# Seven block products in more row pairs of the down and output products, four banks for the first projections, and the key transposes moved in one decoder layer

## The chip, the core and the metric

The kernel runs on one core of a Trainium2 chip. The metric is device time in microseconds (us), the median of several runs. The engines are named by their functions: TensorE (PE, with PEld for its weight loads), VectorE (DVE), ScalarE (ACT), GpSimd (POOL) and SyncE (SP), which issues most DMA transfers.

## What is computed

The reference is one decoder layer over 256 rows of 2048 numbers, in float32:

```python
h = x
h = h + 0.5 * swiglu(rms_norm(h, ffn1_norm), ffn1_w_gate, ffn1_w_up, ffn1_w_down)
p = rms_norm(h, mix_norm) @ w_in
y_rwkv = rwkv7_time_mix(p[..., :RWKV_IN], ...)     # 16 heads of 64
y_lru  = rglru_mix(p[..., RWKV_IN:], ...)          # gated recurrence, then its own rms_norm
h = h + concatenate([y_rwkv, y_lru]) @ w_out
h = h + 0.5 * swiglu(rms_norm(h, ffn2_norm), ffn2_w_gate, ffn2_w_up, ffn2_w_down)
return rms_norm(h, final_norm)
```

The hidden width of the two feed-forward parts is 5632, so a down product sums over 44 row tiles of 128, and the output product over 16.

## The kernel before

**Products.** Every large product is made of three TensorE products, because each float32 operand is held as a high part (a cast) and a low part (the rest): high by high, high by low, low by high (`three`, L146). A weight tile is loaded by SP into `wst`, ScalarE casts it to `whi` (L96 or L115), and VectorE takes the difference into `wlo` (L97 or L116). Three buffers exist of each (`wpool`), and the loading and splitting of weights has a high priority (offset 4000) in the order that a planner makes of the program.

**Pairs.** `rows_times_pairs` (L153) takes two row tiles of weights, 1024 columns wide, at a time. A pair is a two by two by two block product: two row tiles by two halves of the tokens by two halves of 512 columns. A plan string says how each pair is done. In a plain pair (`n`) eight block products are made, 24 matmuls, into four banks `own`. In a pair of kind `S` seven are made, 21 matmuls, from sums of blocks: VectorE makes the sums of weight blocks (L136 to L138), and seven blocks instead of four are split into high and low parts; sums of the activation blocks come from `block_sums` (L297). Four of the seven products go to four more banks, `aux`, which add up over all S pairs and are added in once at the end (`shared_h`, L334).

**Order of stages.** `ffn` runs the gate and the up product in chunks of 1024 columns, both with three S pairs of eight, then the down product in pieces. In the first feed-forward part there are two pieces of 1024 columns with four S pairs of 22 each. In the second there is one such piece and then two pieces of 512 columns without S pairs (`rows_times`, L180). The transposes of the last chunk's hidden values (`hidden_T`, L274, L280) come after the third pair of the first down piece, and they make the activation sums of the last four pairs there.

**Mixing.** `mix_layer` runs eleven projections of `w_in` (`project`, L610; 256-column matmuls at L199 to L201), which take turns on banks 0 to 2, and between them the recurrence work in an order written out by hand (`order`). `keys_T` (L783, transposes at L792) is the last call of step `r`. The rows that come out are split into the tiles `xahi` and `xalo` (`split_rows`, L1022, L1023): row tiles 0 to 3 and 4 to 7 are the recurrence heads, row tiles 8 to 15 the gated part, which is first scaled by its norm (`lru_norm`, L1017 to L1019; L1087). The same tiles hold the projections' input until the last projection has read them.

**Output product.** `mix_out` (L1091) has two halves of 1024 columns, all sixteen row tiles in order, with `rows_times` on banks 0 to 3 and 4 to 7. After each half the result is added to `h` (L1102), transposed (L229) and split for the second feed-forward part (L237, L238).

**End.** The last piece is added to `h` (L428), its squares are summed (L247), it is multiplied by the final gain (L1238), scaled (L1253, L1256) and written out.

Of the kernel before, what the change touches and what calls it, by code (L numbers as in the profile page):

```python
# [15 lines left out]
ALU = mybir.AluOpType  # L16
# [20 lines left out]
class Core:  # L37
# [115 lines left out]
    def rows_times_pairs(self, mat, c0, plan, ids, own, aux, xhi, xlo, sums, hooks):  # L153
# [3 lines left out]
        for at, (kind, p, w) in enumerate(self.pairs(mat, c0, plan, ids)):  # L157
            first, last = at == 0, at == len(plan) - 1
            if kind == "n":
                for kk in range(2):  # L160
                    for t in range(2):
                        x = [v[:, 2 * p + kk, t * P : (t + 1) * P] for v in (xhi, xlo)]
                        for n in range(2):
                            self.three(own[2 * t + n], x, w[kk][n], first and kk == 0, last and kk == 1)
# [12 lines left out]
            for hook in hooks.get(at, ()):  # L177
                hook()
# [63 lines left out]

    def sumsq(self, c0, w, acc, pool):
# [16 lines left out]
def ffn(core, xhi, xlo, rstd, wg, wu, wd, after_first, after_down, fpool, down, rest, back, spare, head=None):  # L260
# [13 lines left out]
    def hidden_T(c0, w, hid, sums=None):  # L274

        for j in range(0, w // P, 2):
# [14 lines left out]
            if sums:  # L291
                if j == 0:
                    raw = fpool.tile([P, 4, 2, S], F32, name=core.name("hsum"), tag="sg")
                nc.scalar.copy(raw[:, j // 2].rearrange("p k s -> p (k s)"), bk)
                block_sums(raw[:, j // 2], *sums(k // 2))

    def block_sums(r, hi, lo):  # L297

        blk = lambda k, t: r[:, k, t * P : (t + 1) * P]
        nc.vector.tensor_tensor(blk(1, 1), blk(0, 1), blk(1, 1), ALU.add)  # L300
        nc.vector.tensor_tensor(blk(0, 1), blk(0, 0), blk(0, 1), ALU.subtract)
        nc.vector.tensor_tensor(blk(0, 0), blk(1, 1), blk(0, 0), ALU.subtract)
        nc.vector.tensor_tensor(blk(1, 0), blk(1, 0), blk(0, 0), ALU.subtract)
        flat = r.rearrange("p k s -> p (k s)")
        nc.scalar.copy(hi, flat)
        nc.vector.tensor_tensor(lo, flat, hi.bitcast(F32), ALU.subtract)
# [26 lines left out]

    def shared_h(aux, tmp, c0):  # L334

        t1, t2, t3, _ = blocks_of(tmp)
        nc.scalar.copy(t1, aux[0])
        nc.vector.tensor_tensor(t2, aux[2], t1, ALU.add)
        nc.vector.tensor_tensor(t3, aux[3], t2, ALU.add)
        for (t, n), parts in (((0, 1), (aux[1], t2)), ((1, 0), (t3,)), ((1, 1), (aux[1], t3)), ((0, 0), (t1,))):  # L340
            hs = core.h[:, t, c0 + n * 512 : c0 + (n + 1) * 512]
            for part in parts:
                nc.vector.scalar_tensor_tensor(hs, part, 0.5, hs, ALU.mult, ALU.add)
# [5 lines left out]
    for c0, w in chunks:  # L349
# [42 lines left out]
        for i, (k, hi, lo) in enumerate(core.weights([(wu, c0, w)], ks)):  # L392
            core.rows_times(ub, xhi, xlo, k, hi, lo, w, i == 0, i == NK - 1)
            if i % 2 and i // 2 in place:
                block_sums(room(i // 2), *sums(place[i // 2]))
# [5 lines left out]
    hsums = spare()  # L401
    first_s = NF // 2 - 4
    bank0 = 0
    for piece, (c0, w) in enumerate(down):
        nb = w // 512
        if w == 1024:
            own, aux = ([core.bank((bank0 + i) % 8) for i in b] for b in (range(4), range(4, 8)))
            bank0 += 4
            plan = DOWN_PLAN[piece]
            number = {"n": iter(range(first_s)), "S": iter(range(first_s, NF // 2))}  # L410
            ids = [next(number[kind]) for kind in plan]
            hooks = {}
            if pending:
                hooks[DOWN_HIDDEN_AT] = [partial(f, sums=hsums) for f in pending]
            pending = []
            tmp = lambda: fpool.tile([P, NT, 1024], F32, name=core.name("dsh"), tag="hid")
            hooks[plan.rindex("S")] = [lambda: shared_h(aux, tmp(), c0)]
            core.rows_times_pairs(wd, c0, plan, ids, own, aux, hT_hi, hT_lo, hsums, hooks)
            db = [own[0:2], own[2:4]]
        else:  # L420
            db = [[core.bank((bank0 + t * nb + n) % 8) for n in range(nb)] for t in range(NT)]
            bank0 += NT * nb
            for i, (k, hi, lo) in enumerate(core.weights([(wd, c0, w)], list(range(NF)))):
                core.rows_times(db, hT_hi, hT_lo, k, hi, lo, w, i == 0, i == NF - 1)
        for t in range(NT):
            for n in range(nb):
                hs = core.h[:, t, c0 + n * 512 : c0 + (n + 1) * 512]
                nc.vector.scalar_tensor_tensor(hs, db[t][n], 0.5, hs, ALU.mult, ALU.add)  # L428
        after_down(piece)
# [8 lines left out]
class Mix:  # L438
# [171 lines left out]
    def project(self, pieces, ntile, xhi, xlo):  # L610
# [3 lines left out]
        for _ in range((ntile + 1) // 2):  # L614
            bks.append(core.bank(self.nproj % 3))
# [410 lines left out]
def mix_layer(core, dram, xhi, xlo, scratch, nslot):  # L1026
    nc = core.nc
    w_in = dram["w_in"][0]
    with ExitStack() as ctx:
# [20 lines left out]
        def receptance(hf):  # L1050
# [40 lines left out]
def mix_out(core, w_out, yhi, ylo, after_half):  # L1091
    nc = core.nc
    half = core.D // 2
    nb = half // 512
    for hf in range(2):
        db = [[core.bank(4 * hf + t * nb + n) for n in range(nb)] for t in range(core.NT)]
        for i, (k, hi, lo) in enumerate(core.weights([(w_out, hf * half, half)], list(range(core.NK)))):
            core.rows_times(db, yhi, ylo, k, hi, lo, half, i == 0, i == core.NK - 1)
        for t in range(core.NT):
            for n in range(nb):  # L1100
                hs_ = core.h[:, t, hf * half + n * 512 : hf * half + (n + 1) * 512]
                nc.vector.tensor_tensor(hs_, hs_, db[t][n], ALU.add)  # L1102
# [10 lines left out]
def kernel(ctx: ExitStack, tc: tile.TileContext, dram: dict, out: bass.AP):  # L1113
# [32 lines left out]
    def xt_pool(stack, name, **kw):  # L1146
# [10 lines left out]
        return [Halves(half(n, 0), half(n, 1)) for n in ("hi", "lo")], half, sums  # L1157

    with ExitStack() as front:
        xa, xa_half, xa_sums = xt_pool(front, "xa")  # L1160
        with ExitStack() as st:
# [32 lines left out]
            def park(hf):  # L1194
# [8 lines left out]
                first_norm, park, fpool, [(0, HD), (HD, HD)], rest, back, xa_sums, head={q: partial(norm_quarter, q + 1) for q in range(3)})  # L1203
# [11 lines left out]
        xb, _, xb_sums = xt_pool(ctx, "xb", **right)  # L1215
# [5 lines left out]
        mix_out(core, dram["w_out"][0], *xa, half_done)  # L1221
    with ExitStack() as st:
        fpool = st.enter_context(tc.tile_pool(name="ffn2", bufs=1, reuse_waits="tile"))
        down = [(0, HD), (HD, HD // 2), (HD + HD // 2, HD // 2)]
        fb = None

        def closing(piece):
            nonlocal fb
            if piece == 0:
# [4 lines left out]
            c0, w = down[piece]  # L1234
            core.sumsq(c0, w, ssq[3][piece], fpool)
# [4 lines left out]
        def rest2():  # L1240
# [6 lines left out]
            lambda: norm_rows(2, 7, fpool), closing, fpool, down, rest2, back2, xb_sums)  # L1247
# [37 lines left out]
```

## Time and profile before

| | |
|---|---|
| median of 3 runs | 1918.13 us (1918.0 to 1919.51) |
| profiled execution | 1919.43 us, span 1917.7 us |
| TensorE | 10197 matmuls, 1885.3 us busy |
| VectorE | 1513.9 us busy |
| ScalarE | 1012.8 us busy |
| granted TensorE clock | 0.994 of full |
| HBM | 351.25 MB read, 187 GB/s |

The profile is of one execution. The span runs from the first to the last instruction. Busy time of TensorE counts overlapping matmuls from the start of each to its modelled end. Lines such as L97 are lines of the kernel before.

### The profile page before, as it was taken

To read this page: it belongs to the slowest core of one execution; us is meant where nothing else is said; L and a number is where in the kernel's file an instruction comes from. 1 tells how busy PE (TensorE), PEld (TensorE's weight loads), DVE (VectorE), ACT (ScalarE), POOL (GpSimd) and SP (SyncE) were. 2 spreads that over 40 slices of the span, in tenths; PEclk is the share of its full clock that TensorE was granted. 3 is DMA by queue.
4 is the path that set the end of the run, shared out by engine and by line. 5 is a ranking of instruction groups with operands and counts; after the bars stand their busy time and mean duration, and the time that the engine had idled before them with its cause. 6 is when DMAs were issued, how large, how long until landed. Compare 5 with 4: busy or idle time off the path is not lost.

```text
span 1917.7 us, 25761 instructions
## 1 busy us (share of the span) xinstructions
PE 1885.3 (98%) x10197; PEld 1591.7 (83%) x10197; DVE 1513.9 (79%) x1952; ACT 1012.8 (53%) x1232; POOL 9.9 (1%) x53
## 2 busy tenths in 40 slices
PE   7999999999999999999999999999999999999997
PEld 6888888888888889898899978888888888888886
DVE  6889999898867567976595775989898989876653
ACT  6555555555544445544454554655556555554443
POOL 0000000000000001000000000000000000000000
PEclk9999999999999999999999999999999999999999
DMA  6565555555655656645243456555655655756653
GB/s 224 180 206 181 197 198 186 208 186 210 240 200 197 220 192 216 179 122 160 82 154 97 132 197 208 189 198 189 206 193 206 216 176 197 262 199 202 208 189 126
DMA packets 130034, 360.79 MB, mean 188 GB/s; under 512 B 20879, under 2 KB 23128, under 8 KB 129784
## 3 DMA queue, kind: packets, MB, share of 16 engines
q1 hardware_dynamic: 129592, 358.08, 55.6%
q8 instruction: 80, 1.31, 0.3%
q10 hardware_dynamic: 320, 1.06, 0.1%
q14 instruction: 42, 0.34, 0.1%
HBM read 351.25 MB, written 7.86 MB: 187 GB/s over the span
## 4 chain that ended last, share of the span: by engine, by line
PE 83%; DVE 10%; DMA 4%; ACT 1%; issue 1%; SPq 0%; DVEq 0%; ACTq 0%
PE bank L149 17%; PE bank L151 17%; PE bank L150 17%; PE bank L190 5%; PE bank L188 5%; PE bank L187 4%; PE bank L200 4%; PE bank L199 4%; PE bank L201 4%; DVE wlo L116 3%; DMA wst<-in_ffn_w_gate_dram 3%; DVE wlo L97 1%; PE bank L280 1%; PE bank L771 1%; PE bank L699 1%
## 5 line engine op out<-in xcount | busy, mean ns | idle before, releaser
L115 ACT CAST whi<-wst 128x1024 fp32r<-128x1024 f32 (+1 forms) x596 | 589.0, 1001 | 542.7 <-PE bank L151 484.8
L116 DVE TENSOR_TENSOR wlo<-wst,whi 128x1024 fp32r<-128x1024 f32 (+1 forms) x596 | 682.6, 1156 | 146.0 <-ACT whi L115 136.9
L97 DVE TENSOR_TENSOR wlo<-wst,whi 128x1024 fp32r<-128x1024 f32 (+2 forms) x197 | 236.7, 1203 | 150.6 <-ACT whi L96 149.5
L96 ACT CAST whi<-wst 128x1024 fp32r<-128x1024 f32 (+2 forms) x197 | 204.1, 1037 | 258.0 <-PE bank L190 115.7
L199 PE MATMUL bank<-xahi,whi 128*128 128x256 f32 x688 | 198.3, 288 | 2.6 <-DVE raw L629 2.6
L201 PE MATMUL bank<-xahi,wlo 128*128 128x256 f32 x688 | 198.8, 289 | 0.2 <-DVE wlo L97 0.2
L200 PE MATMUL bank<-xalo,whi 128*128 128x256 f32 x688 | 198.7, 289 | 0.0
L149 PE MATMUL bank<-whi,xahi 128*128 128x512 f32 x490 | 191.4, 391 | 0.4 <-DVE hTlo L288 0.4
L149 PE MATMUL bank<-whi,xbhi 128*128 128x512 f32 x490 | 191.2, 390 | 0.4 <-DVE hTlo L288 0.4
L150 PE MATMUL bank<-wlo,xahi 128*128 128x512 f32 x490 | 190.8, 389 | 0.0
L150 PE MATMUL bank<-wlo,xbhi 128*128 128x512 f32 x490 | 190.8, 389 | 0.0
L151 PE MATMUL bank<-whi,xalo 128*128 128x512 f32 x490 | 190.6, 389 | 0.0
L151 PE MATMUL bank<-whi,xblo 128*128 128x512 f32 x490 | 190.6, 389 | 0.0
L149 PE MATMUL bank<-whi,hThi 128*128 128x512 f32 x468 | 182.5, 390 | 0.0
L151 PE MATMUL bank<-whi,hTlo 128*128 128x512 f32 x468 | 182.2, 389 | 0.0
L150 PE MATMUL bank<-wlo,hThi 128*128 128x512 f32 x468 | 182.1, 389 | 0.0
L199 PEld LDWEIGHTS bank<-xahi,whi 128*128 128x128 f32 x688 | 133.4, 194 | 5.7 <-DVE raw L629 2.8
L201 PEld LDWEIGHTS bank<-xahi,wlo 128*128 128x128 f32 x688 | 133.4, 194 | 2.4 <-issue 1.2
L200 PEld LDWEIGHTS bank<-xalo,whi 128*128 128x128 f32 x688 | 133.2, 194 | 2.3 <-issue 1.1
L136 DVE TENSOR_TENSOR wst<-wst 128x1024 f32<-128x1024 f32 x72 | 88.1, 1223 | 28.8 <-DMA wst<-in_ffn_w_up_dram 10.5
L149 PEld LDWEIGHTS bank<-whi,xahi 128*128 128x128 f32 x490 | 92.0, 188 | 20.3 <-PE bank L151 0.8
L149 PEld LDWEIGHTS bank<-whi,xbhi 128*128 128x128 f32 x490 | 92.0, 188 | 19.8 <-PE bank L151 0.8
(345 smaller groups left out, 3011.4 us busy)
## 6 DMA issues: line engine op xcount, KB each, us to landing
wst<-in_ffn_w_up_dram SPq DMA_DIRECT2D x88, 1024.0 KB
wst<-in_ffn_w_down_dram SPq DMA_DIRECT2D x88, 1024.0 KB
wst<-in_ffn_w_gate_dram SPq DMA_DIRECT2D x87, 1024.0 KB
wst<-in_w_in_dram SPq DMA_DIRECT2D x40, 1024.0 KB
wst<-in_w_out_dram SPq DMA_DIRECT2D x16, 1024.0 KB
h<-parked SPq DMA_DIRECT2D x4, 1024.0 KB
wst<-in_w_in_dram SPq DMA_DIRECT2D x4, 640.0 KB
h<-in_x_dram SPq DMA_DIRECT2D x4, 512.0 KB
```

Source lines behind the costliest of these rows:

```text
L96: self.last_split = nc.scalar.copy(hi[:, : m * width], src)
L97: nc.vector.tensor_tensor(lo[:, : m * width], src, hi[:, : m * width].bitcast(F32), ALU.subtract)
L115: self.nc.scalar.copy(hv, src)
L116: self.nc.vector.tensor_tensor(lv, src, hv.bitcast(F32), ALU.subtract)
L149: nc.tensor.matmul(out, a[0], b[0], start=first, stop=False)
L150: nc.tensor.matmul(out, a[0], b[1], start=False, stop=False)
L151: self.last_mm = nc.tensor.matmul(out, a[1], b[0], start=False, stop=last)
L188: nc.tensor.matmul(banks[t][n][:, :w], a, wlo[:, c : c + w], start=False, stop=False)
L190: self.last_mm = nc.tensor.matmul(banks[t][n][:, :w], b, whi[:, c : c + w], start=False, stop=last)
L199: nc.tensor.matmul(out, a, xhi[:, k, :], start=first, stop=False, skip_group_check=True)
L200: nc.tensor.matmul(out, a, xlo[:, k, :], start=False, stop=False, skip_group_check=True)
L201: nc.tensor.matmul(out, b, xhi[:, k, :], start=False, stop=last, skip_group_check=True)
```

## The change

- In both down products, all pieces are now 1024 columns wide and have six S pairs of 22. The activation sums of two more pairs are made by `earlier_sums`, at the start of the first piece, from tiles that are already split. The second feed-forward part has two pieces instead of three.
- The output product uses `rows_times_pairs` with three S pairs of eight in each half. Its activation sums are made from the split rows after all of them, in a new pool. Banks 0 to 3 and 4 to 7 serve as `own` and `aux`, exchanged in the second half.
- In the last pair of every such product the matmuls are sorted so that the first 512 columns are finished before the others, and the closing work of the second feed-forward part is split accordingly.
- The first eight bank allocations of the projections go round four banks instead of three.
- `keys_T` is called at the end of step `v` instead of step `r`.

`block_sums` and `shared_h` become methods of `Core`, unchanged but for a scale. The core of the diff (the pools for the new sums are left out):

```diff
             if kind == "n":
-                for kk in range(2):
-                    for t in range(2):
...
+                turns = itertools.product(range(2), range(2), range(2))
+                for kk, t, n in (sorted(turns, key=lambda v: v[2]) if last else turns):
+                    x = [v[:, 2 * p + kk, t * P : (t + 1) * P] for v in (xhi, xlo)]
+                    self.three(own[2 * t + n], x, w[kk][n], first and kk == 0, last and kk == 1)
...
+    def shared_h(self, aux, tmp, c0, scale):
+        nc = self.nc
+        t1, t2, t3 = (tmp[:, i * 512 : i * 512 + 512] for i in range(3))
+        nc.scalar.copy(t1, aux[0])
+        nc.vector.tensor_tensor(t2, aux[2], t1, ALU.add)
+        nc.vector.tensor_tensor(t3, aux[3], t2, ALU.add)
+        for (t, n), parts in (((0, 1), (aux[1], t2)), ((1, 0), (t3,)), ((1, 1), (aux[1], t3)), ((0, 0), (t1,))):
+            hs = self.h[:, t, c0 + n * 512 : c0 + (n + 1) * 512]
+            for part in parts:
+                nc.vector.scalar_tensor_tensor(hs, part, scale, hs, ALU.mult, ALU.add)
...
-    first_s = NF // 2 - 4
+    first_s = NF // 2 - 6
+    def earlier_sums():
+        for n, p in enumerate(range(first_s, first_s + 2)):
+            pair = slice(2 * p, 2 * p + 2)
+            nc.vector.tensor_tensor(hraw[:, n], hT_hi[:, pair, :].bitcast(F32), hT_lo[:, pair, :].bitcast(F32), ALU.add)
+            core.block_sums(hraw[:, n], *hsums(p))
...
+        if piece == 0:
+            hooks[0] = [earlier_sums]
+            hooks[DOWN_HIDDEN_AT] = [partial(f, sums=hsums) for f in pending]
...
-            bks.append(core.bank(self.nproj % 3))
+            bks.append(core.bank(self.nproj % 4 if self.nproj < 8 else (self.nproj - 8) % 3))
...
             TW[hf] = m.invert_blocks(GR[hf], scratch[hf])
-            BKT[hf] = m.keys_T(BK[hf])
 
         def values(hf):
             V[hf] = shifted(2112 + 512 * hf, 16 + 4 * hf, "v")
+            BKT[hf] = m.keys_T(BK[hf])
...
-def mix_out(core, w_out, yhi, ylo, after_half):
+def mix_out(core, w_out, yhi, ylo, after_half, pool):
...
+    for n, p in enumerate(spairs):
+        raw = pool.tile([P, 2, core.S], F32, name=core.name("ysum"), tag="ysum", bufs=2)
+        pair = slice(2 * p, 2 * p + 2)
+        nc.vector.tensor_tensor(raw, yhi[:, pair, :].bitcast(F32), ylo[:, pair, :].bitcast(F32), ALU.add)
+        core.block_sums(raw, sums[:, n, 0, :], sums[:, n, 1, :])
...
+        own, aux = ([core.bank((4 * hf + i) % 8) for i in b] for b in (range(4), range(4, 8)))
+        core.rows_times_pairs(w_out, hf * half, OUT_PLAN, range(core.NK // 2), own, aux, yhi, ylo, of,
+                              {OUT_PLAN.rindex("S"): [lambda: core.shared_h(aux, tmp(), hf * half, 1.0)]})
...
+OUT_PLAN = "nSnSnSnn"
-DOWN_PLAN, DOWN_HIDDEN_AT = ("nnnnnnSnnnSnnnSnnnSnnn", "nnnSnnnnSnnnnSnnnnSnnn"), 2
+DOWN_PLAN, DOWN_HIDDEN_AT = ("nnnnSnnSnnSnnSnnSnnSnn", "nnSnnSnnSnnSnnSnnSnnnn"), 2
```

## Rows read from the trace of the kernel before

**Rows 1.** The page, part 1: engine, busy us, share of the span, instructions.
```profile
PE 1885.3 (98%) x10197; PEld 1591.7 (83%) x10197; DVE 1513.9 (79%) x1952; ACT 1012.8 (53%) x1232; POOL 9.9 (1%) x53
```
**Rows 2.** Matmuls by start, us long: tiles 0, 8 of half 0; half 1; next stage.
```profile
1098.25 0.40 PE L187 MATMUL bank<-whi,xahi 128*128 128x512 f32 x1
...
1128.51 0.39 PE L187 MATMUL bank<-whi,xahi 128*128 128x512 f32 x1
...
1150.27 0.39 PE L187 MATMUL bank<-whi,xahi 128*128 128x512 f32 x1
...
1195.69 0.39 PE L187 MATMUL bank<-whi,xbhi 128*128 128x512 f32 x1
```
**Rows 3.** Busy time by stretch: a down piece, then around the output product.
```profile
core 0: us, PE busy (x) PEld busy (x) DVE busy (x) ACT busy (x) POOL busy (x), PEclk, DMA share, GB/s
615.00:731.00 116.00, 116.00 (x521) 96.26 (x520) 77.63 (x81) 56.72 (x62) 1.36 (x13) 1.00 0.57 193
1080.00:1094.00 14.00, 14.00 (x112) 13.36 (x110) 14.00 (x12) 7.49 (x9) 0.00 (x0) 1.00 0.28 86
1094.00:1136.00 42.00, 40.94 (x195) 33.05 (x195) 38.39 (x61) 24.02 (x34) 0.11 (x1) 1.00 0.48 156
...
1151.00:1195.00 44.00, 44.00 (x203) 36.42 (x202) 23.72 (x27) 19.39 (x24) 0.00 (x0) 1.00 0.66 216
```
**Rows 4.** VectorE by group, 1094 to 1136 us: x, busy us, mean ns, idle before.
```profile
L97 DVE TENSOR_TENSOR wlo<-wst,whi 128x1024 fp32r<-128x1024 f32 x13 | 15.7, 1208 | 1.8 <-ACT whi L96 1.7
L1087 DVE SCALAR_TENSOR_TENSOR xc<-xc,pc,lss 128x256 f32<-128x256 f32 x8 | 3.4, 475 | 0.0
```
**Rows 5.** VectorE on row tiles 7, 8 to 10 and 12 to 15 of the output product.
```profile
1119.21 0.43 DVE L1023 TENSOR_TENSOR xalo<-y,xahi 128x256 fp32r<-128x256 f32 x1 [0.47 <-ACT xahi L1022]
...
1128.45 1.09 DVE L1023 TENSOR_TENSOR xalo<-xc,xahi 128x256 fp32r<-128x256 f32 x3
...
1134.05 1.42 DVE L1023 TENSOR_TENSOR xalo<-xc,xahi 128x256 fp32r<-128x256 f32 x4
```
**Rows 6.** VectorE around one S pair of a down piece, in order of time.
```profile
536.77 1.23 DVE L136 TENSOR_TENSOR wst<-wst 128x1024 f32<-128x1024 f32 x1 [0.99 <-DMA wst<-in_ffn_w_down_dram]
537.91 1.22 DVE L116 TENSOR_TENSOR wlo<-wst,whi 128x1024 fp32r<-128x1024 f32 x1
539.04 0.69 DVE L137 TENSOR_TENSOR wst<-wst,wst 128x512 f32<-128x512 f32 x1
539.65 1.82 DVE L116 TENSOR_TENSOR wlo<-wst,whi 128x512 fp32r<-128x512 f32 x2
541.38 0.69 DVE L138 TENSOR_TENSOR wst<-wst,wst 128x512 f32<-128x512 f32 x1
542.71 1.23 DVE L116 TENSOR_TENSOR wlo<-wst,whi 128x1024 fp32r<-128x1024 f32 x1 [0.64 <-ACT whi L115]
```
**Rows 7.** VectorE on activation sums and the last hidden tile's low part, first down piece.
```profile
511.92 0.48 DVE L300 TENSOR_TENSOR hsum<-hsum 128x128 f32<-128x128 f32 x2
512.32 0.49 DVE L301 TENSOR_TENSOR hsum<-hsum 128x128 f32<-128x128 f32 x2
...
520.68 0.68 DVE L306 TENSOR_TENSOR xasum<-hsum,xasum 128x512 fp32r<-128x512 f32 x1
...
521.49 0.68 DVE L288 TENSOR_TENSOR hTlo<-bank,hThi 128x512 fp32r<-128x512 f32 x1
```
**Rows 8.** Transposes of keys (L792) and of hidden values (L280), TensorE.
```profile
507.70 1.91 PE L280 MATMUL bank<-ident,hid 128*128 128x128 f32 x16
941.64 0.60 PE L792 MATMUL bank<-ident,bk 128*128 128x128 f32 x4
```
**Rows 9.** Waits of TensorE, whole span: us in total, times, longest.
```profile
PE bank L199 <- DVE raw L629: 2.6, 1, 2.6
...
PE bank L699 <- ACT bk L714: 1.5, 1, 1.5
```
**Rows 10.** VectorE at the end.
```profile
1904.97 1.37 DVE L428 SCALAR_TENSOR_TENSOR h<-bank,h 128x512 f32<-128x512 f32 x2 [5.17 <-PE bank L190]
```

More of the change, by code (lines that the diff above doesn't have):

```diff
@@ L332, in shared @@
         nc.vector.tensor_tensor(d22, aux[1], d21, ALU.add)
[L334 to L343, printed above, removed]
     pending = []
@@ L394, in ffn @@
             if i % 2 and i // 2 in place:
-                block_sums(room(i // 2), *sums(place[i // 2]))
+                core.block_sums(room(i // 2), *sums(place[i // 2]))
         for t in range(NT):
@@ L400, in ffn @@
     back()
-    hsums = spare()
-    first_s = NF // 2 - 4
-    bank0 = 0
-    for piece, (c0, w) in enumerate(down):
[L405 to L426, printed above, removed]
@@ new lines, in ffn @@
+    four, (hraw, two) = spare(), more()
+    first_s = NF // 2 - 6
+    hsums = lambda p: four(p) if p >= NF // 2 - 4 else tuple(two[:, i, p - first_s, :] for i in range(2))
+    def earlier_sums():
[3 more added lines that the diff above has]
+            core.block_sums(hraw[:, n], *hsums(p))
+    for piece, (c0, w) in enumerate(down):
+        own, aux = ([core.bank((4 * piece + i) % 8) for i in b] for b in (range(4), range(4, 8)))
+        plan = DOWN_PLAN[piece]
+        number = {"n": iter(range(first_s)), "S": iter(range(first_s, NF // 2))}
+        ids = [next(number[kind]) for kind in plan]
+        hooks = {}
+        if piece == 0:
+            hooks[0] = [earlier_sums]
+            hooks[DOWN_HIDDEN_AT] = [partial(f, sums=hsums) for f in pending]
+        tmp = lambda: fpool.tile([P, 1536], F32, name=core.name("dsh"), tag="hid")
+        hooks[plan.rindex("S")] = [lambda: core.shared_h(aux, tmp(), c0, 0.5)]
+        core.rows_times_pairs(wd, c0, plan, ids, own, aux, hT_hi, hT_lo, hsums, hooks)
+        for n in range(2):
+            for t in range(NT):
@@ L427, in ffn @@
                 hs = core.h[:, t, c0 + n * 512 : c0 + (n + 1) * 512]
-                nc.vector.scalar_tensor_tensor(hs, db[t][n], 0.5, hs, ALU.mult, ALU.add)
-        after_down(piece)
+                nc.vector.scalar_tensor_tensor(hs, own[2 * t + n], 0.5, hs, ALU.mult, ALU.add)
+            after_down(piece, n)
 C = 64
@@ L1155, in sums @@
             return lambda p: tuple(t[:, p % 4, :] for t in tiles)
-        return [Halves(half(n, 0), half(n, 1)) for n in ("hi", "lo")], half, sums
+        return [Halves(half(n, 0), half(n, 1)) for n in ("hi", "lo")], half, sums, pool
     with ExitStack() as front:
-        xa, xa_half, xa_sums = xt_pool(front, "xa")
+        xa, xa_half, xa_sums, xa_pool = xt_pool(front, "xa")
         with ExitStack() as st:
@@ L1202 @@
             ffn(core, *xa, rstd[0], dram["ffn1_w_gate"][0], dram["ffn1_w_up"][0], dram["ffn1_w_down"][0],
-                first_norm, park, fpool, [(0, HD), (HD, HD)], rest, back, xa_sums, head={q: partial(norm_quarter, q + 1) for q in range(3)})
+                first_norm, park, fpool, [(0, HD), (HD, HD)], rest, back, xa_sums, more, head={q: partial(norm_quarter, q + 1) for q in range(3)})
         mix_layer(core, dram, *xa, scratch, NSLOT)
@@ L1219, in half_done, with more2, closing @@
             nc.sync.dma_start(out=parked[hf], in_=core.h[:, :, hf * HD : (hf + 1) * HD])
-        mix_out(core, dram["w_out"][0], *xa, half_done)
+        with tc.tile_pool(name="ysums", bufs=1, reuse_waits="tile") as ypool:
+            mix_out(core, dram["w_out"][0], *xa, half_done, ypool)
     with ExitStack() as st:
         fpool = st.enter_context(tc.tile_pool(name="ffn2", bufs=1, reuse_waits="tile"))
-        down = [(0, HD), (HD, HD // 2), (HD + HD // 2, HD // 2)]
+        down = [(0, HD), (HD, HD)]
         fb = None
-        def closing(piece):
+        def more2():
+            raw = xb_pool.tile([P, 4, 2, S], F32, name="hsum2", tag="lo0")
+            return raw, xb_pool.tile([P, 2, 2, 512], F32R, name="hsum2b", tag="hi0")
+        def closing(piece, n):
             nonlocal fb
+            if piece == 0 and n == 0:
+                return
             if piece == 0:
```

57 lines of the change are left out of this document (30 added, 27 removed).

## The prediction

> **What bounds the kernel now.** I read the page first. TensorE is busy 98% of the span, VectorE 79% and ScalarE 53% [rows 1], so the end is set by TensorE nearly everywhere, and the first question is what one matmul is worth. A row gives a 512-column matmul 0.39 to 0.40 us, but that is its length, and the next one starts before it ends. The timeline gives the distance: row tile 8 of the first half of the output product starts at 1128.51 and the second half at 1150.27 [rows 2]; eight row tiles of twelve matmuls lie between them, so one matmul costs 21.76/96 = 0.2267 us of TensorE's time. The reader is to see that pricing by length would overstate every saving by 1.7 times.
>
> The second view is busy time by stretch [rows 3], because the 79% of VectorE is a mean over unlike stages. In a down piece VectorE works 77.63 of 116 us, and there is room. Ahead of the output product it has none: 14.00 of 14.00 us from 1080 to 1094, and 38.39 of 42.00 from 1094 to 1136. Only behind that does it fall to half (23.72 of 44).
>
> The third view is what VectorE does in those 42 us and who needs it. Thirteen of its instructions split weights, 15.7 us [rows 4]; all else is the end of the mixing, which makes the rows that the output product multiplies. TensorE starts on row tile 8 at 1128.51 [rows 2], and VectorE starts on the low parts of row tiles 8 to 10 at 1128.45 [rows 5]. The first half of the output product thus already runs with no margin behind VectorE. What is added to VectorE here is paid by TensorE.
>
> **What is removed.** An S pair has 21 matmuls instead of 24. Down: the first feed-forward part goes from 8 S pairs to 12, the second from 4 to 12 (a piece without S pairs has as many matmuls in two halves of 512 columns as in one of 1024). Output: from 0 to 6. That is 12 + 24 + 18 = 54 matmuls, or 54 x 0.2267 = 12.2 us; 8.2 of it in the down products and 4.1 in the output product. The Trainium skill, TensorE: Matmul & The Clock Gate, section "Wait — 56ns, not 53.3ns?", puts the distance of warm 512-column matmuls at 215.7 ns. By it the 54 would be worth 11.6 us; the row's 0.2267 is near and decides.
>
> **What an S pair adds.** From start to start [rows 6]: weight sums 1.14 (L136), 0.61 (L137) and about 0.61 (L138); splits 1.13 for 1024 columns three times and 0.60 for 512 once: 1.14 + 0.61 + 0.61 + 3 x 1.13 + 0.60 = 6.35 us of VectorE. A plain pair has two splits, 2.26. So each S pair adds 4.1 us to VectorE while it takes 0.68 from TensorE. The Trainium skill, VectorE: DVE Perf Modes, section on the TRN2 errata, gives a float32 sum of N numbers per partition (N+151)/0.96 ns, 1224 and 691 here. The rows' lengths agree (1.22, 0.69). Priced by length an S pair would be 4 x 1.224 + 3 x 0.691 = 6.97 us and three of them 1.9 us more than by the starts; I keep the starts, since the next instruction begins before the former ends.
>
> Activation sums of a pair: one addition (as L306, 0.61 from start to start), four small ones at 0.20 when two pairs are interleaved (0.40 for two [rows 7]) and the low part, 0.61: 2.0 us; 0.28 each for the small ones when alone makes 2.4.
>
> **Down products: −8.2.** Per three pairs VectorE gets 2 x 2.26 + 6.35 = 10.9 us, TensorE 2 x 5.44 + 4.76 = 15.6. The cover is there, and would be gone only if S pairs followed each other at less than 6.35 us. The start of the first piece is the one place to doubt. Two more pairs of sums (4.0 us) come into it, and the first S pair stands at index 4 instead of 6. Its `aux` banks are those in which the last chunk's hidden values are transposed, 507.70 on [rows 8]. The last of them was still read by VectorE at 521.49 [rows 7], while the S pair would want it at about 507.70 + 1.8 + 5.4 + 12 x 0.2267 = 517.6. That is up to 4.5 us late in each part; what does not need that bank (products t2 and t4, the next plain pair) can go ahead. I take 0.5 for each, 1.0 in all, bounds 0 and 9.
>
> **Output product, first half.** Up to 1136 VectorE did all of the mixing's end and 13 weight splits, 13 x 1.13 = 14.7 us, which is row tiles 0 to 12. In the new order the last S pair of the half is the sixth pair, row tiles 10 and 11. Before it can end, VectorE must do three plain and three S pairs, 3 x 2.26 + 3 x 6.35 = 25.8, and three activation sums, 6.0. The added work is 25.8 − 14.7 + 6.0 = 17.1 us. The window has 42.00 − 38.39 = 3.6 us of idle time [rows 3]. If all of it is filled, the sixth pair's weights are ready at 1136 + 13.5 = 1149.5; if none, at 1153.1. TensorE then has the last six matmuls (1.4) and pairs seven and eight, 48 x 0.2267 = 10.9: the half ends at 1161.8 to 1165.4 instead of 1150.27, 11.5 to 15.1 later. Two bounds lie outside. If the work on row tiles 12 to 15 goes behind, 1.7 of L1087 [rows 4] and 1.4 of L1023 [rows 5], it is 8.5 later. If the first S pair's activation sums wait until all rows are split, as the program's order has it, TensorE stands behind its second pair: VectorE needs 23.7 (the mixing's end) + 2.3 + 6.4 + 2.0 = 34.4 us, so it goes on at 1128 to 1132, and then pairs that VectorE must still split one behind the other (6.35 + 2.0 before an S pair against TensorE's 5.4 of cover) follow: some 20 later. I take 15: VectorE works in a fixed order, and its splits wait for ScalarE and for buffers as they do now (0.64 in [rows 6], 1.8 in [rows 4]).
>
> **Output product, second half.** Nine matmuls less, −2.0. Its first S pair puts `aux` into banks 0 to 3, which hold the first half's result until four additions (4 x 0.61) and the splits of its transposes (8 x 0.44) are done, 5.9 us of VectorE, beside the pair's own 6.35; TensorE has 5.4 + 1.8 us to do meanwhile. Between 0 and 5 us of wait, I take 2.5: together +0.5. `shared_h`, eight VectorE instructions of 0.61 or 4.9 us, is hidden behind pairs seven and eight of each half (10.9 us, in which VectorE has 4.5 of splits); without that cover it would cost its 4.9.
>
> **Mixing.** The 2.6 us wait of a projection for its bank [rows 9] stands where step r1's second bank was k1's first. It is so in the new numbering too (k1 gets 0 and 1, r1 gets 2 and 0), so it stays. Four banks free the earlier projections from such neighbours, which cost nothing visible there beside the 1.5 us wait for ScalarE [rows 9]. The key transposes (groups of four in 0.60 us [rows 8]) and ScalarE's copies of them are as many as before, and are read only in the recurrence step far behind; in step v they stand behind the value projection's matmuls. I take −0.5, bounds −2.6 and +1.5.
>
> **End.** The first 512 columns are now finished 12 matmuls, 2.7 us, before the last one; their closing takes VectorE 4 x 0.61 = 2.4 [rows 10], so 0, at most 0.5.
>
> **Sum.** −8.2 + 1.0 + 15.0 + 0.5 − 0.5 = +7.8. The profiled execution took 1919.43 (span 1917.7), so 1927.2; its distance to the median, 1.3, taken off: **1926 us**, slower by 0.4%. About 0.2%, 3.8 us, is what a measurement here can tell from no change.
>
> **Rivals.** *VectorE's added work finds room* (the other side): the planner fits sums and splits so that the first half ends no later. Then the whole 12.2 is seen, 1906 us. For it speaks that gate and up stages bear three S pairs of eight with no such mixing beside them; against it that 38.39 of 42 us are taken and that row tile 8 has no margin. It decides for faster from the point where the first half ends less than 3.4 us late (then the sum is −3.8). Chance 0.20. *Half the cost*: late by 4 to 11 us, as in the lower bound, and the down products pay for it: 1914 to 1922, chance 0.16. *Sums behind all rows*: the first S pair stands until the mixing is over, 20 to 27 us: 1931 to 1938; for it speaks that they are written last, against it that the planner fills idle moments. Chance 0.18. *Bank wait at the down start*: 4.5 us in both parts on top of the forecast: 1934, chance 0.05. *The forecast*: 11 to 19 us late, 1922 to 1930, chance 0.41.
>
> The range is 1909 to 1938: it leaves out most of the first rival and nothing much above; the forecast's own range is 1922 to 1930. Slower by over 0.2%: 0.41 + 0.18 + 0.05 = 0.64, less 0.01 at its edge; within: 0.15 and faster: 0.22, the first rival and the edge of the second.
>
> **What would show it.** From the first output matmul to the end of the first half, 52.0 us before [rows 2], about 67; TensorE waiting there for `wlo` or the new sums, and VectorE full until some 50 us after the half's start. Second half about 46, against 45.4 [rows 2]. The second feed-forward part's last 1024 columns 2.7 to 4 us shorter. The prediction is wrong if the first half takes under 56 us, or if the down pieces show waits of more than a few us.

## The result, and the profile after

The changed kernel took 1943.83 us (median of 4 runs, 1940.45 to 1948.07) against 1918.82 (4 runs) for the kernel before on the same chip: ratio 1.0131, 95% interval 1.0118 to 1.0145. It is slower, as forecast, but by 25 us where I had 8, and it lies above my range. The profiled execution took 1946.04 us (span 1944.3).

From first matmul to first matmul the stages lasted, in us:

| stage | before | after | difference | my term |
|---|---|---|---|---|
| first part, gate and up | 491.38 | 491.13 | −0.25 | 0 |
| first down product | 237.69 | 236.10 | −1.6 | −2.2 |
| mixing | 369.19 | 368.80 | −0.4 | −0.5 |
| output product, first half | 52.02 | 74.73 | +22.7 | +15.0 |
| output product, second half | 45.42 | 52.50 | +7.1 | +0.5 |
| second part, gate and up | 471.32 | 475.72 | +4.4 | none |
| second down product | 238.60 | 233.64 | −5.0 | −4.9 |
| end | 12.06 | 11.67 | −0.4 | 0 |

(My −8.2 + 1.0 for the down products is split here by its 4 and 8 added pairs of three matmuls and half a microsecond of wait each.)

The page's first part, to be held against [rows 1]: VectorE has 102 us more to do, TensorE does fewer matmuls and is busy for longer.

```profile
PE 1887.1 (97%) x10143; PEld 1585.1 (82%) x10143; DVE 1615.9 (83%) x2108; ACT 1048.3 (54%) x1278; POOL 9.7 (0%) x53
```

The start of the output product, of its seventh pair, of its second half and of the next stage, which answer to [rows 2]:

```profile
1096.03 0.40 PE L149 MATMUL bank<-whi,xahi 128*128 128x512 f32 x1
...
1159.88 0.39 PE L149 MATMUL bank<-whi,xahi 128*128 128x512 f32 x1
...
1170.76 0.39 PE L149 MATMUL bank<-whi,xahi 128*128 128x512 f32 x1
...
1223.26 0.47 PE L186 MATMUL bank<-whi,xbhi 128*128 128x512 f32 x1
```

Busy time in the two halves of the output product, first of the kernel before (the same columns as [rows 3]), then of the changed one:

```profile
core 0: us, PE busy (x) PEld busy (x) DVE busy (x) ACT busy (x) POOL busy (x), PEclk, DMA share, GB/s
1098.25:1150.27 52.02, 50.96 (x223) 40.62 (x221) 41.08 (x63) 28.25 (x38) 0.00 (x0) 1.00 0.59 200
1150.27:1195.69 45.42, 45.42 (x209) 37.46 (x208) 25.14 (x29) 19.93 (x24) 0.00 (x0) 1.00 0.65 211
```

```profile
1096.03:1170.76 74.73, 54.44 (x213) 41.56 (x212) 65.20 (x104) 36.29 (x49) 0.11 (x1) 0.86 0.42 141
1170.76:1223.26 52.50, 47.58 (x210) 37.12 (x208) 42.48 (x54) 25.27 (x31) 0.00 (x0) 0.97 0.60 200
```

The reader is to see two things. VectorE's work in the first half rose by 24.1 us (65.20 − 41.08), and the half became 22.7 us longer. And TensorE was idle for 20.3 us of it (74.73 − 54.44), where it had been idle for 1.1; what it did took 3.5 us more although nine matmuls (2.0 us) were gone, at a mean granted clock of 0.86.

The waits of TensorE over the whole span, to be held against [rows 9]. One wait carries most of the idle time:

```profile
PE bank L149 <- ACT ysums L251: 14.9, 1, 14.9
PE bank L149 <- ACT whi L115: 4.4, 3, 2.7
...
PE bank L150 <- DVE wlo L116: 2.3, 3, 0.8
...
PE bank L149 <- DVE hTlo L311: 1.8, 1, 1.8
...
PE bank L198 <- DVE raw L628: 0.7, 1, 0.7
```

The timeline of TensorE at that wait:

```profile
1118.69 1.46 PE L1007 MATMUL bank<-gate,ones 128*128 128x256 f32 x6
1135.02 0.79 PE L149 MATMUL bank<-whi,ysums 128*128 128x512 f32 x1 [14.87 <-ACT ysums L251]
1135.61 0.63 PE L150 MATMUL bank<-wlo,ysums 128*128 128x512 f32 x1
1136.04 0.63 PE L151 MATMUL bank<-whi,ysums 128*128 128x512 f32 x1
1136.47 0.63 PE L149 MATMUL bank<-whi,ysums 128*128 128x512 f32 x1
```

and of VectorE meanwhile: row tile 3 was split at 1108.54, the last two row tiles at 1128.55, and only then come the first sums (L1099) and, beside them, the odd 512-column weight split of the first S pair:

```profile
1108.54 0.42 DVE L1022 TENSOR_TENSOR xalo<-y,xahi 128x256 fp32r<-128x256 f32 x1
...
1128.55 0.82 DVE L1022 TENSOR_TENSOR xalo<-xc,xahi 128x256 fp32r<-128x256 f32 x2
1129.29 1.28 DVE L1099 TENSOR_TENSOR ysum<-xahi,xalo 128x512 f32<-128x512 f32 x2
1130.49 0.69 DVE L116 TENSOR_TENSOR wlo<-wst,whi 128x512 fp32r<-128x512 f32 x1
```

That is the picture of my rival *sums behind all rows*. The weight split has nothing to do with the sums, and no weight load was issued between 1104.4 and 1141.7, so its weights had long been asked for. That is the hint that something else than order holds both back: they lie in one pool (`ysums`), which takes the place of the mixing's tiles.

### The profile page after: what moved, and what is told of

It is laid out like the page before. It is cut to its first block, busy times and chain, and to the rows that moved or that the text cites. A ratio compares the mean times of both kernels' runs of the same rounds, so it can differ in the third digit from the quotient of the medians.

```text
span 1944.3 us, 25843 instructions
## 1 busy us (share of the span) xinstructions
PE 1887.1 (97%) x10143; PEld 1585.1 (82%) x10143; DVE 1615.9 (83%) x2108; ACT 1048.3 (54%) x1278; POOL 9.7 (0%) x53
## 4 chain that ended last, share of the span: by engine, by line
PE 68%; DVE 15%; DMA 12%; ACT 2%; issue 2%; SPq 0%; DVEq 0%; ACTq 0%
PE bank L150 16%; PE bank L151 16%; PE bank L149 16%; DVE wlo L116 7%; DMA wst<-in_ffn_w_gate_dram 6%; DMA wst<-in_ffn_w_up_dram 4%; PE bank L199 3%; PE bank L198 3%; PE bank L200 3%; PE bank L189 2%; PE bank L187 2%; PE bank L186 1%; DVE wst L136 1%; DMA wst<-in_w_out_dram 1%; DVE wlo L97 1%
## 5 line engine op out<-in xcount | busy, mean ns | idle before, releaser
L115 ACT CAST whi<-wst 128x1024 fp32r<-128x1024 f32 (+1 forms) x708 | 696.5, 998 | 625.6 <-PE bank L151 471.9
L116 DVE TENSOR_TENSOR wlo<-wst,whi 128x1024 fp32r<-128x1024 f32 (+1 forms) x708 | 807.3, 1152 | 140.2 <-ACT whi L115 132.0
L150 PE MATMUL bank<-wlo,xahi 128*128 128x512 f32 x588 | 230.4, 392 | 1.8 <-DVE wlo L116 1.6
L151 PE MATMUL bank<-whi,xalo 128*128 128x512 f32 x588 | 229.6, 392 | 0.0
L149 PE MATMUL bank<-whi,hThi 128*128 128x512 f32 x584 | 227.5, 390 | 0.0
L151 PE MATMUL bank<-whi,hTlo 128*128 128x512 f32 x584 | 227.3, 389 | 0.0
L150 PE MATMUL bank<-wlo,hThi 128*128 128x512 f32 x584 | 227.3, 389 | 0.0
L96 ACT CAST whi<-wst 128x1024 fp32r<-128x1024 f32 (+2 forms) x121 | 124.0, 1027 | 147.7 <-PE bank L199 105.0
L97 DVE TENSOR_TENSOR wlo<-wst,whi 128x1024 fp32r<-128x1024 f32 (+2 forms) x121 | 143.7, 1190 | 57.8 <-ACT whi L96 57.2
L150 PEld LDWEIGHTS bank<-wlo,xahi 128*128 128x128 f32 x588 | 111.1, 189 | 26.9 <-DVE wlo L116 3.9
```

What stands on the lines that cost most here:

```text
L96: self.last_split = nc.scalar.copy(hi[:, : m * width], src)
L97: nc.vector.tensor_tensor(lo[:, : m * width], src, hi[:, : m * width].bitcast(F32), ALU.subtract)
L115: self.nc.scalar.copy(hv, src)
L116: self.nc.vector.tensor_tensor(lv, src, hv.bitcast(F32), ALU.subtract)
L149: nc.tensor.matmul(out, a[0], b[0], start=first, stop=False)
L150: nc.tensor.matmul(out, a[0], b[1], start=False, stop=False)
```

## The experiments

Fourteen runs. Ratios are to the kernel before, run on the same chip. Stages that an edit doesn't touch differ between executions too: the first part's gate and up products took 487.1 to 491.4 us in them, the mixing 366.7 to 371.8, so that a stage difference below some 4 us says nothing of itself there. The output product is steadier: plain, it took 97.4 in every run.

**Parts alone.** First the changed kernel with the old output product, then the old kernel with the new output product.

```
-mix_out(..., ypool): rows_times_pairs(w_out, ..., OUT_PLAN, ...)
+mix_out(...):        rows_times(db, yhi, ylo, k, hi, lo, half, ...)   # as before
```

> The changed kernel with the output product put back to its old form (all pairs plain, no sums, no pool of its own); the down products, the banks of the first projections and the keys' transposes stay as changed. If the stages add, it keeps -1.6 us of the first down product, -0.4 of the mixing and -5.0 of the second down product, and its output product takes the 97.4 us of before. Theory A (the 4.4 us that the second feed-forward part's gate and up products lost are a consequence of the output product): that stage returns to about 471.3 us, total 1911 to 1912, ratio about 0.996. Theory B (they come with the changed down products or their tiles): the stage stays at about 475.7 us, total about 1915 to 1916, ratio about 0.998.

Measured: 1916.68 us, ratio 0.9980 (0.9968 to 0.9991). Output product 97.39, second down product 233.58, and gate and up of the second part 479.51. Theory A is out.

> The kernel before with the output product's change alone. If the stages add, the output product takes 127 us, and nothing else is gained: 1918.8 + 29.8 = 1948.6 us; with Theory A of the gate and up products (their 4.4 us follow from the output product) 1953 us, ratio 1.016 to 1.018; with Theory B 1948.6 us, ratio 1.0155. If the loss needs the two parts together, it is nearer to the kernel before.

Measured: 1949.9 us, ratio 1.0164 (1.0145 to 1.0182); output product 127.22, gate and up of the second part 472.34. So the output product's edit alone makes the loss, the rest of the change gains a little, and the 4.4 us of gate and up come with the rest.

**Order or space.** Two edits of the changed kernel:

```
+        with core.tc.high_priority(offset=4000):          # first run: the sums raised
             raw = pool.tile(...); ...; core.block_sums(raw, ...)
```
```
-    sums = pool.tile([P, len(spairs), 2, 512], F32R, name="ysums")   # second run
+    his, los = (room.tile([P, 4, 512], F32R, ..., tag=f"{n}1") for n in ("hi", "lo"))
-    core.bpool = pool        # the odd weight split's pool
+    core.bpool = None        # it takes a tile of the weights' pool
```

> The changed kernel, but the sums of the activations stand 4000 places ahead in the planner's order, as the weight splits do. Theory ORDER (the sums come behind the last row splits because they are written behind them): the sums of the first seven-product pair, whose rows are there from about 1108 us on, are made before the last rows, the wait of 14.9 us goes or falls under 4 us, and the output product takes 105 to 113 us: total 1925 to 1932. Theory SPACE (the pool in which sums and one weight split lie takes the place of the mixing's tiles and cannot be written before the last of those is read): nothing moves, the wait stays at 14 to 16 us, total 1940 to 1948.

Measured: 1940.22 us, ratio 1.0108 (1.0089 to 1.0126); the wait 12.5 us, ending at 1135.00 (1135.02 in the changed kernel), and the sums still behind all row splits. Order alone does nothing for them. The first half took 71.80, although the wait was still there.

> The changed kernel, but the sums lie in tiles on the other side of the memory (the second halves of the next part's activations, which are written only after the output product), their raw block in a small pool opened ahead of the mixing, and the odd weight split in the weights' own pool; their order in the text is as in the changed kernel. Theory SPACE: the first pair's sums and the odd split come ahead of the last row splits, the wait of 14.9 us falls under 4 us and the half-rate matmuls behind it go; what is left of the 127 us is VectorE's own time, 105 to 113 us, total 1925 to 1932. Theory ORDER: the sums still come last and the total stays at 1940 to 1948. Theory LOAD (VectorE has no time for them, wherever they lie): the wait is only spread over other places, the stage stays over 118 us, total over 1936.

Measured: 1937.87 us, ratio 1.0096 (1.0078 to 1.0115); the wait 9.4 us, output product 121.0 (73.96 and 47.06). SPACE's forecast was not met, and ORDER's wasn't either; LOAD's bounds were (stage over 118, total over 1936), though the wait was not spread: 9.4 us of it stayed in one place. The sums did come forward, 1109.95 instead of 1129.29, so space had held them; but VectorE took until 1123.99 for the first block, among its other work, and ScalarE's cast of it (L252) stands behind the casts of the last rows:

```profile
1123.71 0.28 DVE L250 TENSOR_TENSOR ysum<-ysum 128x128 f32<-128x128 f32 x1
```
```profile
1131.38 0.80 ACT L1022 CAST xahi<-xc 128x256 fp32r<-128x256 f32 x2 [1.00 <-DVE xc L1087]
1132.09 0.61 ACT L252 CAST ysums<-ysum 128x512 fp32r<-128x512 f32 x1
```

**Both out of the way.** The sums in the mixing's own tiles, written right behind the rows that they sum:

```
+        for p in (1, 3):
+            sums.append(m.row_sums(p, xhi, xlo))   # tiles from m.slot(...)
         m.lru_norm()
```

> The changed kernel, but the sums of the activations lie in the mixing's own tiles, which are kept open until the output product is over, and are written in the text right behind the rows that they sum (two of the three ahead of the rows of the linear recurrence); the odd weight split lies in the weights' pool. Space and order are thus both out of the way. Theory WAIT (the loss is the one wait for sums and what follows from it): the output product falls to 97 to 102 us, total 1914 to 1920. Theory LOAD (VectorE has no time for 17 us more of work ahead of 1136 us, wherever it stands; my +15 without the wait): the waits move to the splits and rows behind, the stage takes 108 to 114 us, total 1925 to 1931. Theory HALF (some of it fits): 103 to 107 us, total 1920 to 1924.

Measured: 1935.32 us, ratio 1.0090 (1.0075 to 1.0104). The first S pair's sums are there at 1122.44, after a wait of 1.36 us. And the output product takes 124.72 us, 72.84 and 51.88. The waits of TensorE are now small and many; the four largest rows of this stage, then the wait for the third S pair's sums, and the stretch between the two waits for sums:

```profile
PE bank L150 <- ACT whi L116: 4.4, 5, 1.3
PE bank L150 <- ACT ysums L252: 4.1, 2, 2.8
PE bank L694 <- DVE parts_rs L689: 4.0, 1, 4.0
PE bank L151 <- DVE wlo L117: 2.0, 2, 1.2
```
```profile
1150.26 0.80 PE L150 MATMUL bank<-whi,ysums 128*128 128x512 f32 x1 [2.76 <-ACT ysums L252]
```
```profile
1122.00:1150.00 28.00, 22.00 (x90) 16.43 (x90) 27.12 (x44) 17.69 (x26) 0.00 (x0) 0.96 0.53 167
```

WAIT and HALF are out. With the long wait gone the first half is only 1.9 us shorter (74.73 to 72.84), and the run with raised sums was at 71.80 with the wait in place. (This run also puts the odd weight split into the three buffers of the weights, which may cost something.) By the ratios the whole kernel gained some 8 us; 2.5 of it lie in the output product, the others in stages that differ as much between executions. VectorE was busy for 27.12 of the 28 us between the two waits. LOAD is left, though the stage is longer than I gave it (108 to 114).

**The dose.** If VectorE's load is the cause, work taken from it must come back as time. Two more runs on top of the last one. The first leaves out the sums of weight blocks in the output product, and GpSimd fills their tile with zeros; the second leaves out the activation sums too, and blocks of the raw rows stand in for them:

```
-                    nc.vector.tensor_tensor(t[:, 0:2], ...)   # and t[:, 2], t[:, 3]
+                    nc.gpsimd.memset(tt, 0.0)                 # output product only
```
```
-        ...; self.core.block_sums(raw, t[:, 0:512], t[:, 512:1024])
+        return tuple(v[:, 2 * p : 2 * p + 2, :].rearrange(...) for v in (yhi, ylo))
```

> The run with early sums, but in the output product the three sums of the weights of a seven-product pair are left out; GpSimd fills their tile with zeros instead, so buffers and matmuls are the same. That takes 2.36 us of VectorE from each of six pairs, 7.1 us per half. Theory LOAD (the first half is as long as VectorE needs): its 72.8 us fall by 5.5 to 7.1, to 65.5 to 67.5, and the whole by 6 to 11 us. Theory BUFFERS (the splits wait for buffers that TensorE gives back late, and VectorE's busy time is only along): the first half stays at 70 to 73 us.

> The run without weight sums, and the sums of the activations left out too; blocks of the raw rows stand in for them in the matmuls. That takes another 6.0 to 7.5 us of VectorE from the first half, 13 to 14.6 in all against the run with early sums. Theory LOAD: the first half takes 58 to 61 us against 72.8, about one us for each us of VectorE taken out. Theory BUFFERS: it stays over 68 us. If there is a remainder over the 49.9 us that the plain half would take with nine matmuls less, it is the splits of 512 and 1024 columns that a seven-product pair has more than a plain one (1.7 us each, 5.2 for three) and the buffers.

Measured: 1924.93 us, ratio 1.0040 (1.0018 to 1.0061), and 1916.80 us, ratio 1.0001 (0.9989 to 1.0013). The first half of the output product with early sums, without weight sums, and without any sums, in this order, one fence each:

```profile
1093.15:1165.99 72.84, 58.57 (x214) 43.91 (x212) 63.63 (x103) 35.29 (x48) 0.10 (x1) 0.84 0.44 145
```
```profile
1097.29:1159.55 62.26, 56.62 (x215) 42.40 (x213) 55.34 (x92) 34.86 (x48) 5.43 (x3) 0.89 0.49 169
```
```profile
1093.59:1148.02 54.43, 51.66 (x214) 38.06 (x213) 46.49 (x70) 33.20 (x45) 5.45 (x3) 1.00 0.54 174
```

VectorE's busy time goes 63.63, 55.34, 46.49; the half 72.84, 62.26, 54.43. So 17.1 us less of VectorE gave 18.4 us, 1.07 us for each, and in the first step more than that (10.6 for 8.3), while the granted clock rose from 0.84 to 0.89 and 1.00. BUFFERS, which wanted 68 us or more with the same matmuls and buffers, falls. LOAD holds in kind, but both halves are shorter than it had them (65.5 to 67.5, and 58 to 61). One rival is left: each step takes from the program not only VectorE's time but also instructions that TensorE's operands wait for, one behind the other (load, sum, cast, low part). These runs don't tell the two apart; extra VectorE work that nobody waits for would. The second halves took 51.88, 45.17 and 48.54: there the first step gave 6.7 us and the second took 3.4 back, for a reason that I don't know. The remainder, 54.43 against 49.98 (52.02 less nine matmuls), is 4.5 us, which the two added weight splits of each S pair (5.2 us of VectorE for three) would fill.

**Where the mixing is over.** S pairs in the second half alone (`OUT_PLANS = "nnnnnnnn", "nnSnSSnn"`), gate and up with their old matmul order:

> The changed kernel with the matmul order of the gate and up products taken back, and seven-product pairs in the second half of the output product alone (plan n n S n S S n n), where the mixing is over; the first half is plain. If VectorE's load at the end of the mixing is the cause of the output product's loss, the first half takes 52 us as before and the second 43.4 to 45 (nine matmuls or 2.0 us less, up to 1.5 of waits): output product 95.5 to 97.5, total 1904 to 1909, ratio 0.992 to 0.995. If seven-product pairs with sums cost the output product more than they save wherever they stand, the second half takes over 47 us and the total is over 1910.

Measured: 1914.15 us, ratio 0.9984 (0.9973 to 0.9996). First half 52.14; second half:

```profile
1145.96:1193.12 47.16, 45.05 (x202) 35.38 (x200) 41.04 (x51) 25.05 (x31) 0.00 (x0) 1.00 0.61 202
```

1.7 us more than the plain half, with VectorE at 41.04 of 47.16. The 43.4 to 45 us of the first theory were missed, and the bounds of the second (over 47, total over 1910) were met. So the output product gains from S pairs in neither half, also where the first half is plain.

**Gate and up of the second part.** `rows_times_pairs`, in which the change reorders the last plain pair's matmuls, is called by the gate and up products too. The order taken back there (in both feed-forward parts), on top of the run with the old output product:

```
-                for kk, t, n in (sorted(turns, key=lambda v: v[2]) if last else turns):
+                for kk, t, n in (sorted(turns, key=lambda v: v[2]) if last and by_half else turns):
```

> The run with the output product in its old form, and one more edit taken back: the matmuls of the last plain pair go column half by column half in the down products alone, and in the old order in the gate and up products, which call the same function. Theory TURNS (this shared edit moves one weight split of VectorE by one place in every chunk of the second part, and TensorE then waits for it): the second part's gate and up products return from 479.5 (475.7 in the changed kernel) to 471 to 472 us; total 1906 to 1909, ratio 0.993 to 0.995. Theory TILES (the gate and up products lose by the changed tiles and plans of the down products): they stay at 475 to 480 us, total 1912 to 1917. The second down product keeps its 233.6 us in both.

Measured: 1909.37 us, ratio 0.9955 (0.9942 to 0.9969); the stage 471.47 us against 479.51, as TURNS had it. Then the reverse, that order as the only edit of the kernel before:

> The kernel before with one edit of the change alone: the order of the matmuls of the last plain pair, column half by column half, for all calls of that function. Theory TURNS: the second part's gate and up products go from 471.3 to 475 to 480 us and nothing else moves; total 1922 to 1927, ratio 1.002 to 1.004. If the loss there needs other edits too, the stage stays at 471 to 472.5 us and the ratio is within 0.999 to 1.001.

Measured: 1917.48 us, ratio 0.9999 (0.9990 to 1.0009); the stage 470.98. Alone it costs nothing, so TURNS as it stands falls. Three more runs on one chip:

> The run with the output product in its old form and the shared matmul order, a second time, on the same chip as the next one. Theory COMPANY (the shared order costs together with the changed down products): gate and up of the second part over 475 us again, ratio 0.997 to 0.999. Theory VARIES (that stage varies by some us between executions, and the first run had a bad one): 471 to 474 us, ratio within 0.001 of the next kernel's.

> The same with the shared order taken back in the gate and up products, a second time. COMPANY: 471 to 472 us there, ratio 0.994 to 0.996, at least 0.0015 under the kernel beside it. VARIES: 471 to 474 us, and the ratio within 0.001 of the kernel beside it.

> The changed kernel whole, with the shared order taken back in the gate and up products alone. COMPANY: gate and up of the second part return from 475.7 to 471 to 472.5 us, total 1938 to 1941, ratio 1.010 to 1.0115 against the changed kernel's 1.0131. VARIES: 472 to 476 us, ratio 1.012 to 1.0145.

Measured: 1914.31 us, ratio 0.9986 (0.9974 to 0.9997); 1908.11, 0.9953 (0.9940 to 0.9965); 1944.73, 1.0138 (1.0123 to 1.0153). The stage, in the same order, one fence each:

```profile
1192.82:1667.39 474.57, 472.23 (x2115) 387.83 (x2114) 427.89 (x508) 272.52 (x318) 0.00 (x0) 1.00 0.57 199
```
```profile
1192.83:1664.33 471.50, 471.27 (x2116) 388.12 (x2114) 428.50 (x508) 273.21 (x319) 0.00 (x0) 1.00 0.58 200
```
```profile
1216.10:1693.28 477.18, 472.50 (x2115) 388.00 (x2114) 427.46 (x507) 272.94 (x319) 0.00 (x0) 1.00 0.57 198
```

Beside the old output product the order costs 6.2 us by the medians (1914.31 − 1908.11), and the ratios are those of COMPANY; the stage itself differs by 3.1 us in this pair of profiles (8.0 in the pair before) and stays just under COMPANY's 475. In the whole changed kernel taking the order back returns nothing, so it is not the cause there. In all three the work is the same and VectorE is busy for 90% of the stage; what differs is how long TensorE stands (2.3, 0.2 and 4.7 us).

**Banks and keys.** The kernel before with these two edits alone:

> The kernel before with the four banks of the first projections and the moved transposes of the keys alone. Predicted -0.5 us for the mixing (bounds -2.6 and +1.5). The mixing took 369.2 us in the kernel before, 368.8 in the changed kernel, 370.5 in a run without this edit, and 366.9 to 371.8 in runs with it, so a run of 367 to 370 decides little; the wait of a projection for its bank should fall from 2.6 to 0.7 us, and the ratio stand at 0.998 to 1.000.

Measured: 1916.96 us, ratio 1.0001 (0.9992 to 1.0010); mixing 367.77 us. TensorE's wait for the bank in this run, and in the run with the matmul order alone, which has the old banks:

```profile
PE bank L199 <- DVE raw L629: 0.7, 1, 0.7
```
```profile
PE bank L198 <- DVE raw L628: 3.2, 1, 3.2
```

The wait goes, and the time doesn't: the mixing of the second run took 367.92.

## Why the prediction was wrong, step by step

**Right: the bound and the sign.** That the first half of the output product runs without margin behind VectorE, and that TensorE pays for what is added there, is what the dose shows, but for the rival named there. The down products' term was right as well: −7.2 forecast, −6.6 measured, and the trace shows no wait of TensorE in them.

**Wrong: "Output product, first half", +15.** It measured +22.7. The amount of work was near: three S pairs at 4.1, the activation sums at 6.0 and `shared_h` at 4.9 make 23.2 us of VectorE in the half, and the trace after has 24.1 more. What failed is the path. I let TensorE wait last for the sixth pair's weights, and put the wait for the first S pair's activation sums outside, as a bound. In the changed kernel that wait set the half: at 1135.02 TensorE still had 141 of the half's 183 matmuls before it, 32.0 us at 0.2267, and the half ended 35.7 us later. The sixth pair was over at 1159.88, 63.9 us behind the half's start, where I had 52.7 to 56.2. Behind it pairs seven and eight took 10.88 us, as forecast and without a wait, so that `shared_h` beside them cost nothing in this half.

With the sums made early it is still +20.8 (72.84 − 52.02). There the sixth pair waits for its own activation sums until 1150.26, 57.1 us behind the half's start, where I had its weights at 51.3 to 54.9. Twelve matmuls are left then and take 4.8 us, at first 0.43 us apart; I had six left, at 1.4 us. So the sums were in the amount of work, but my path had TensorE wait for weights alone.

**The rival "sums behind all rows".** Its picture came, a wait until 1135.02, and the size of its price (20 to 27 us in the half; 22.7). Its reason didn't: raising the sums in the order changed nothing, and moving their tiles brought them forward. The pool's place in memory held them, not the order of the text. As the only cause it fell too, since without the wait the half is 1.9 us shorter: other waits came in its place.

**Wrong: "Output product, second half", +0.5.** It measured +7.1. I had priced a wait for banks of 0 to 5 us. The trace shows 0.5 us of that kind (`xblo`) and a wait for weights. VectorE, SP's loads and TensorE there:

```profile
1171.37 1.22 DVE L116 TENSOR_TENSOR wlo<-wst,whi 128x1024 fp32r<-128x1024 f32 x1
...
1173.11 1.22 DVE L116 TENSOR_TENSOR wlo<-wst,whi 128x1024 fp32r<-128x1024 f32 x1
...
1179.15 1.65 DVE L237 SCALAR_TENSOR_TENSOR xblo<-bank,gT,xbhi 128x256 fp32r<-128x256 f32 x4
1182.95 1.23 DVE L136 TENSOR_TENSOR wst<-wst 128x1024 f32<-128x1024 f32 x1 [2.15 <-DMA wst<-in_w_out_dram]
```
```profile
1172.61 2.10 SPq L126 DMA_DIRECT2D wst<-in_w_out_dram  x2
```
```profile
1180.94 0.47 PE L149 MATMUL bank<-whi,xahi 128*128 128x512 f32 x1 [0.49 <-DVE xblo L237]
...
1184.55 1.20 PE L149 MATMUL bank<-whi,xahi 128*128 128x512 f32 x4 [2.67 <-ACT whi L115]
1186.57 0.80 PE L150 MATMUL bank<-wlo,xahi 128*128 128x512 f32 x1 [0.82 <-DVE wlo L116]
```

An S pair takes two of the three `wst` tiles, one for the weights and one for their sums. VectorE was done with two tiles at 1172.59 and 1174.33, and SP issued the next loads at 1172.61 and 1174.35; the load before was issued at 1161.4. The weights were there at 1182.95, and TensorE stood for 2.67 us. Against the plain half less nine matmuls (43.38) the half is 9.1 us longer: 4.9 of it are idle time (52.50 − 47.58), 1.6 are seven matmuls from 1186.57 on that took 3.15 us instead of 1.59, and the other 2.6 I can't assign. That is read from the trace; no run with more tiles tested it. Nor is it shown that the first half's lateness is behind it: with the sums elsewhere the first half took 73.96 and the second only 47.06, and S pairs in the second half alone cost 1.7.

**Missing: gate and up of the second part, +4.4.** No step had it; I took the new matmul order for an edit of the down products' end, and didn't see that gate and up call the same function. The runs show that this order costs some 6 us in one company and nothing in two others, so I can't name one edit. What is common to the cases is a stage in which VectorE is busy for 90% of the time. And the stage differs by as much without any edit: one and the same kernel, the change with the old output product, had 479.51 and 474.57 in its two profiles. Which part of the change tips it in the changed kernel stays open.

**Mixing, −0.5.** It measured −0.4, but that is luck: the wait of 2.6 us that I said stays went to 0.7, and alone the edit is worth nothing (ratio 1.0001).

**Sum.** −0.25 − 1.6 − 0.4 + 22.7 + 7.1 + 4.4 − 5.0 − 0.4 = +26.6, the distance of the two profiled executions (1946.04 − 1919.43).

The best kernel of the study is the change without its output product and with the old matmul order in gate and up: 1909.37 and 1908.11 us on two chips, ratios 0.9955 and 0.9953.

## What to carry to other kernels

Price a trade between two engines stage by stage: seven products for eight are a gain where VectorE has room (the down products) and a loss where it has none. In the first half of the output product each us of work taken from VectorE gave back about one. Ask of added work not only how much it is but who waits for it first: the activation sums stood in TensorE's way, and `shared_h` beside the half's last two pairs did not make that half longer. Before you blame the one long wait in a profile, remove it and see what the stage takes: here, with a wait of 14.9 us gone, the half was 1.9 shorter. And look up every caller of a function that an edit touches.

## What the runs showed of the hardware

TensorE's stand has a price behind it. After 14.87 us without work it ran its next matmuls 0.43 us apart (1136.04 to 1136.47) instead of 0.23, at a granted clock of 0.56 from 1135 to 1139, which is mostly the 1.2 GHz level:

```profile
1121.00:1135.00 14.00, 0.00 (x0) 0.00 (x0) 13.40 (x30) 4.72 (x11) 0.00 (x0) 0.64 0.21 75
1135.00:1139.00 4.00, 3.98 (x10) 3.07 (x11) 3.77 (x10) 1.36 (x3) 0.00 (x0) 0.56 0.72 262
```

The Trainium skill, TensorE: Matmul & The Clock Gate, section "Wait — 56ns, not 53.3ns?", gives 426.7 ns from start to start for 512 columns at 1.2 GHz; the trace agrees.

The clock may also be why the first step of the dose gave back more than it took from VectorE: the half's mean clock rose from 0.84 to 0.89 in it. That link is read from the clock column alone.
